# A 3×3 convolution in row pairs: the shared products of two blocks put side by side, and the last stores cut smaller

## The chip, the cores and the metric

The kernel runs on one core of a Trainium2 chip. The metric is the device time of one execution in microseconds (us); lower is better. Three timed runs of the kernel before gave 131.26, 131.46 and 131.46 us, a median of 131.46 us.

## The reference

`x` is 16 images of 64 channels, 64×64, fp32; `weight` is 128×64×3×3, nine tenths of it zeros; the output is 16×128×64×64 fp32 (33.6 MB). The reference skips zero weights, which changes nothing in the sum, so what is computed is a plain 3×3 convolution with zero padding:

```python
x_pad = np.pad(x, ((0, 0), (0, 0), (pad, pad), (pad, pad)), mode='constant')
...
output[b, co] += weight[co, ci, kh, kw] * x_pad[b, ci, kh:kh+h, kw:kw+w]
```

## The kernel before

**The arithmetic.** Two neighbouring output rows 2r and 2r+1 read the four input rows 2r−1 to 2r+2. With the kernel rows w0, w1, w2, both outputs hold the term w1·(x[2r]+x[2r+1]). The kernel computes this once, as the *shared product* P. What is left for the even row is E = w0·x[2r−1] + (w2−w1)·x[2r+1], done as one product over 128 partitions (two input rows of 64 channels each), and for the odd row likewise O = (w0−w1)·x[2r] + w2·x[2r+2]. The output rows are E+P and O+P.

**The tiling.** Images go in eight pairs; a pair's two images lie in partitions 0–63 and 64–127 of `xs` (bf16, converted by the loading DMA). A pair is cut into four blocks of 16 output rows, so there are 32 blocks, b = 0 to 31. For each block:

- `row_sum` (L106) adds neighbouring input rows into `ss[b % 2]`; POOL does it from block 2 on.
- `fill` (L108, copies at L130) builds `win[b % 2]`, in which each image takes 128 partitions: four half-windows per block. ACT copies two of them (both of image 1), POOL one, DVE one.
- TensorE runs three products of six matmuls each (L291). P is two images side by side, each on 64 of the 128 rows of the array, so its six matmuls run as three simultaneous pairs. E and O use all 128 rows, six matmuls one after the other. P goes to `ps_p[b % 2]` (two buffers), E to `ps_e`, O to `ps_o` (one buffer each).
- ACT copies `ps_p` to `pcs[b % 2]` (L211). DVE adds it to `ps_e` and then to `ps_o` and writes `os` (L244). I call these two the evictions of E and of O.
- After a pair's last block DVE writes a small `mark` (L252), on which the SP queue starts the store of `os`.

**The order.** There is no scheduler: every engine's program is written out by hand, with semaphores. TensorE runs a hardware loop of 16 turns, two blocks in a turn: P0 E0 O0 P1 E1 O1 (I number the blocks of a turn 0 and 1). Semaphores `s`, `xg`, `xd`, `xa` count row sums and window fills (by POOL, DVE, ACT), `e` and `o` count evictions, and `q` and `p` count finished products. At a turn's end TensorE takes two turns' worth of counts back with six semaphore decrements (L320):

```python
product(ps_e, lambda n: win[l][:, n, 0:16:2, :], EVEN,
    [[("e", l + 1), ("xg", l + 1), ("xd", l + 1)], [("xa", 2 * l + 2)]], "q")
product(ps_o, lambda n: win[l][:, n, 1:16:2, :], ODD, [[("o", l + 1)], []], "q")
```

So E of a block waits until E of the block before has been evicted; between the two lie O and P.

ACT's program for block b is: keep P(b) in `pcs`, fill one half-window of block b+1, fill one of block b+2. POOL's is: fill its half-window of block b, form the row sum of block b+1, and after blocks 4, 8, 12, 16 and 20 start a load of a later pair. DVE's is: evict E, evict O, fill its half-window of block b+2.

**The stores.** `os` has three buffers of a pair each. Pairs 0 to 6 are stored as one 4 MB DMA each (L145), pair 7 as two halves of 2 MB (L151), after blocks 29 and 31.

Of the kernel before, what the change touches and what calls it, by code (L numbers as in the profile page):

```python
# [17 lines left out]
def kernel(  # L18
# [11 lines left out]

    nc = tc.nc

    B, C_IN, H, W = x.shape
# [14 lines left out]
    def tiles(n, shape, dtype, name):  # L50
        return [pool.tile(shape, dtype, name=f"{name}{k}") for k in range(n)]
# [2 lines left out]
    win = tiles(2, [128, 2, 16, W], BF16, "win")  # L54
    os = tiles(N_O, [C_OUT, 2, H, W], FP32, "o")
    ss = tiles(2, [128, 8, W], BF16, "s")
    pcs = tiles(2, [128, 2, 8, W], FP32, "pc")
    w_sb = pool.tile([C_OUT, C_IN * KH * KW], FP32, name="w_sb")
    x_head = pool.tile([128, HEAD, W], FP32, name="x_head")
    ident = pool.tile([128, 128], BF16, name="ident")  # L60
    idle_rhs = pool.tile([128, 512], BF16, name="idle_rhs")
    w_bf = pool.tile([C_OUT, 3, 3, 2, C_IN], BF16, name="w_bf")
    wT = pool.tile([128, 3, 3, C_OUT], BF16, name="wT")
    mark = pool.tile([128, 1], FP32, name="mark")
    ps_p = [psum_pool.tile([128, 2, 8, W], FP32, name=f"ps_p{k}") for k in range(2)]
    ps_e = psum_pool.tile([128, 2, 8, W], FP32, name="ps_e")
    ps_o = psum_pool.tile([128, 2, 8, W], FP32, name="ps_o")
# [16 lines left out]
    def out_of(p):  # L84
        return out[2 * p : 2 * p + 2].rearrange("n o h w -> o n h w")
# [12 lines left out]

    X_LANDS = {0: 16, 1: 16, 2: 16, 3: 16, 4: 32, 5: 32, 6: 32, 7: 48}
    HEAD_R, HEAD_C, HEAD_Q = 6, 5, 3  # L100
    R_OF = {p: HEAD_R + p + 1 for p in range(NP - 1)}

    FIRST_E = ("q", HEAD_Q + 1)

    def row_sum(eng, b, rows):
        return eng.tensor_tensor(out=ss[b % 2], in0=rows[:, 0:16:2, :], in1=rows[:, 1:16:2, :], op=ADD)  # L106
# [1 line left out]
    def fill(copy, b, n, upper, name, *more):  # L108

        p, r0 = b // 4, 16 * (b % 4)  # L110
        src = slice(64 * n, 64 * n + 64)
        dst = slice(64 * upper, 64 * upper + 64)
        first = r0 - 1 + 2 * upper
        parts = []
        if p == 0 and first < HEAD:
            a, z = max(first, 0), min(first + 16, HEAD)
            parts.append((x_head[src, a:z, :], a - first))
        if p or first + 16 > HEAD:
            a, z = (first, first + 16) if p else (max(first, HEAD), first + 16)
            parts.append((xs[src, p, a + 1 : z + 1, :], a - first))  # L120
        for k, (rows, q) in enumerate(parts):
            waits = []
            if k == 0:
                waits.extend(more or [("q", HEAD_Q + 2 * (b - 2) + 2)] * (b >= 2))
                waits.extend([("xh", 16)] * (b < 2))
            if b in (1, 2) and k == 1:
                waits.append((x_sem(0), X_LANDS[0]))
            if b and b % 4 == 0:
                waits.append((x_sem(p), X_LANDS[p]))
            inst = after(copy(out=win[b % 2][dst, n, q : q + rows.shape[1], :], in_=rows), *waits)  # L130
            if k == len(parts) - 1:
                inst.then_inc(S(name), 1)

    with tc.tile_critical(no_gpsimd_drain=True):  # L134
        with nc.Block(no_gpsimd_drain=True) as block:  # L135

            @block.sync
            def _(sp):
                sp.dma_start(  # L139
                    out=w_sb, in_=weight.rearrange("o i kh kw -> o (i kh kw)")  # L140
                ).then_inc(S("w"), 16)
                sp.dma_start(out=x_head, in_=pair(0)[:, 0:HEAD, :]).then_inc(S("xh"), 16)
                for p in range(NP - 1):
                    after(
                        sp.dma_start(out=out_of(p), in_=os[p % N_O]), ("r", R_OF[p])  # L145
                    ).then_inc(S(f"st{p % N_O}"), 16)
                p = NP - 1
                for h in range(2):
                    rows = slice(32 * h, 32 * h + 32)
                    after(  # L150
                        sp.dma_start(  # L151
                            out=out_of(p)[:, :, rows, :], in_=os[p % N_O][:, :, rows, :]
                        ),
                        ("r", HEAD_R + NP + h),
                    ).then_inc(S("st7" if h else f"st{p % N_O}"), 16)

            @block.gpsimd
            def _(gp):
                def load(p, a, b, *waits):
                    after(  # L160
                        gp.dma_start(out=xs[:, p, a + 1 : b + 1, :], in_=pair(p)[:, a:b, :]), *waits  # L161
                    ).then_inc(S(x_sem(p)), 16)

                load(0, HEAD, H)
                gp.memset(ident, 0.0).then_inc(S("id"), 1)
                after(
                    gp.affine_select(
                        out=ident,
                        in_=ident,
                        compare_op=mybir.AluOpType.not_equal,  # L170
                        fill=1.0,
                        base=0,
                        pattern=[[-1, 128]],
                        channel_multiplier=1,
                    ),
                    ("id", 1),
                ).then_inc(S("id"), 1)
                for p in range(1, 4):
                    load(p, 0, H)
                load(4, 0, CUT)  # L180

                AT = {
                    4: (4, CUT, H, ("r", R_OF[0])),
                    8: (5, 0, H, ("r", R_OF[1])),
                    12: (6, 0, H, ("r", R_OF[2])),
                    16: (7, 0, 32, ("r", R_OF[3])),
                    20: (7, 32, H, ("r", R_OF[4])),
                }
                for b in range(1, NB):
                    fill(gp.tensor_copy, b, 0, 0, "xg", ("q", HEAD_Q + 2 * (b - 1) + 1))  # L190
                    if b + 1 < NB:
                        p, r0 = (b + 1) // 4, 16 * ((b + 1) % 4)
                        waits = [(x_sem(p), X_LANDS[p])] if r0 == 0 or b == 1 else []
                        if b == 1:
                            waits.append(("p", 2))
                        after(row_sum(gp, b + 1, xs[:, p, r0 + 1 : r0 + 17, :]), *waits).then_inc(S("s"), 1)
                    if b in AT:
                        load(*AT[b])

            @block.scalar  # L200
            def _(act):
                after(act.copy(out=w_bf[:, MID, :, 1, :], in_=w_row(1)), ("w", 16)).then_inc(S("c"), 1)  # L202
                act.copy(out=w_bf[:, EVEN, :, 0, :], in_=w_row(0)).then_inc(S("c"), 1)
                act.copy(out=w_bf[:, ODD, :, 1, :], in_=w_row(2)).then_inc(S("c"), 1)
                after(act.copy(out=wT[:, MID], in_=wps(MID)), ("q", 1)).then_inc(S("c"), 1)
                after(act.copy(out=wT[:, ODD], in_=wps(ODD)), ("q", 3)).then_inc(S("c"), 1)

                fill(act.copy, 0, 0, 0, "xg")
                fill(act.copy, 0, 1, 1, "xa")
                for b in range(NB):  # L210
                    after(act.copy(out=pcs[b % 2], in_=ps_p[b % 2]), ("p", b + 1)).then_inc(S("c"), 1)  # L211
                    if b == 0:
                        fill(act.copy, 1, 1, 1, "xa", FIRST_E)
                    if b + 1 < NB:
                        fill(act.copy, b + 1, 1, 0, "xa")
                    if b + 2 < NB:
                        fill(act.copy, b + 2, 1, 1, "xa")

            @block.vector
            def _(dve):  # L220
# [8 lines left out]
                after(dve.tensor_copy(out=wT[:, EVEN], in_=wps(EVEN)), ("q", 2)).then_inc(S("r"), 1)  # L229
                for b in range(2):  # L230
                    after(row_sum(dve, b, x_head[:, 16 * b : 16 * b + 16, :]), ("xh", 16)).then_inc(S("s"), 1)
                    fill(dve.tensor_copy, b, 0, 1, "xd")
                    if b == 0:
                        fill(dve.tensor_copy, b, 1, 0, "xa")
                for b in range(NB):
                    p, r0 = b // 4, 16 * (b % 4)
                    for k, src in enumerate((ps_e, ps_o)):
                        waits = [("q", HEAD_Q + 2 * b + k + 1)]
                        if k == 0:
                            waits.append(("c", HEAD_C + b + 1))  # L240
                            if b % 4 == 0 and p >= N_O:
                                waits.append((f"st{p % N_O}", 16 * (p // N_O)))
                        after(
                            dve.tensor_tensor(  # L244
                                out=os[p % N_O][:, :, r0 + k : r0 + 16 : 2, :], in0=src, in1=pcs[b % 2], op=ADD
                            ),
                            *waits,
                        ).then_inc(S("eo"[k]), 1)
                    if b + 2 < NB:
                        fill(dve.tensor_copy, b + 2, 0, 1, "xd")  # L250
                    if b % 4 == 3 or b == NB - 3:
                        dve.memset(mark, 0.0).then_inc(S("r"), 1)  # L252

            @block.tensor
            def _(pe):
# [46 lines left out]

                with pe.Fori(0, NB // TURN, 1):
                    for l in range(TURN):
                        product(ps_p[l], lambda n: ss[l], MID, [[("s", l + 1)], []], "p")
                        product(
                            ps_e,
                            lambda n: win[l][:, n, 0:16:2, :],
                            EVEN,
                            [  # L310
                                [("e", l + 1), ("xg", l + 1), ("xd", l + 1)],
                                [("xa", 2 * l + 2)],
                            ],
                            "q",
# [4 lines left out]
                    for name, n in (("s", 1), ("xa", 2), ("xd", 1), ("xg", 1), ("e", 1), ("o", 1)):  # L319
                        pe.sem_inc(S(name), -n * TURN)  # L320

    sixteen = nc.sync.to_reg(16)
    done = {f"st{k}": 16 * len([p for p in range(NP) if p % N_O == k]) for k in range(N_O)}
    for name in sorted(done, key=lambda k: (done[k], k)):
        nc.sync.wait_ge(S(name), nc.sync.to_reg(done[name]), synchronizes=[nc.sync.lower_ap(o[:]) for o in os])
    nc.sync.wait_ge(S("st7"), sixteen, synchronizes=[nc.sync.lower_ap(o[:]) for o in os])


# [28 lines left out]
```

## Time and profile before

| what | value |
|---|---|
| median of three runs | 131.46 us |
| the profiled execution's own time | 131.17 us |
| its span, first to last instruction | 129.4 us |
| PE busy | 117.0 us (90%) |
| ACT / DVE / POOL busy | 99.7 / 98.2 / 72.2 us |
| evictions, DVE (L244) | 64 of 1.22 us |
| keeps of P, ACT (L211) | 32 of 1.01 us |
| window fills (L130) | ACT 1.03, POOL 1.03, DVE 0.44 us in the mean |
| row sums, POOL (L106) | 30 of 1.15 us |
| stores of 4 MB, issue to landing | 15.6 us (median of 7) |
| stores of 2 MB, issue to landing | 8.7 us (median of 2) |

The profiled execution's time is 1.77 us above its span; this lies around the first and last instruction. PE's busy time is no measure of how near TensorE is to its limit, since matmuls overlap in it. The chain that ended last (PE 82% of the span) says more: from about 12 us to 119 us every step of it is a product on TensorE, and the next product follows it at once. The last 9 us of the span hold no engine's work, only DMA.

### The profile page before, as it was taken

What the parts mean: (1) busy time and instruction counts of PE and PEld (TensorE: products, weight loads), DVE (VectorE), ACT (ScalarE), POOL (GpSimd) and SP (SyncE); (2) the same over time, 40 slices, a digit from 0 to 9 for tenths busy, and PEclk for the clock granted to TensorE, in tenths of its full rate; (3) what the DMA queues carried; (4) which work ended last, traced back from release to release, by engine and by line L of the source; (5) the groups of instructions that cost most, each with busy time, mean ns of one, the idle gap of its engine ahead of it and who ended that gap; (6) DMA issues with size and microseconds to landing.
All of it is one profiled execution on the core that took longest, in us unless ns stands there. A gap on an engine that the chain in (4) does not pass through costs nothing.

```text
span 129.4 us, 1814 instructions
## 1 busy us (share of the span) xinstructions
PE 117.0 (90%) x599; PEld 44.0 (34%) x599; DVE 98.2 (76%) x116; ACT 99.7 (77%) x104; POOL 72.2 (56%) x78
## 2 busy tenths in 40 slices
PE   5997999999999999999999999999999999998000
PEld 2332343334333333333334333433333333333000
DVE  2589988888888888888888888888888888886200
ACT  3689988899888888888888889988888888863000
POOL 5406765675567666866667556755566666630000
PEclk9999999999999999999999999999999999999955
DMA  4999999999999999999999999999999916999994
GB/s 110 354 229 208 220 218 206 252 360 305 333 375 405 279 319 319 375 337 339 324 372 413 372 338 429 442 333 379 376 415 410 431 56 284 446 405 405 410 436 208
DMA packets 4179, 42.79 MB, mean 331 GB/s; under 512 B 336, under 2 KB 336, under 8 KB 1104
## 3 DMA queue, kind: packets, MB, share of 16 engines
q1 hardware_dynamic: 2736, 34.90, 65.8%
q0 software_dynamic: 1440, 7.86, 29.4%
q14 instruction: 3, 0.02, 0.0%
HBM read 17.07 MB, written 33.55 MB: 391 GB/s over the span
## 4 chain that ended last, share of the span: by engine, by line
PE 82%; DVE 5%; DMA 4%; issue 1%; SPq 0%; DVEq 0%
PE ps_e L291 34%; PE ps_o L291 31%; PE ps_p L291 17%; DMA x_head<-in_x_dram 4%; DVE win L130 2%; DVE o L244 2%; DVE s L106 1%; SPq L139 0%; SPq L352 0%; SPq L134 0%; DVEq L135 0%
## 5 line engine op out<-in xcount | busy, mean ns | idle before, releaser
L130 ACT COPY win<-xs 64x1024 bf16<-64x1024 bf16 (+2 forms) x61 | 62.7, 1028 | 12.3 <-PE ps_o L291 12.2
L244 DVE TENSOR_TENSOR o<-ps_e,pc 128x1024 f32<-128x1024 f32 x32 | 39.2, 1225 | 14.7 <-PE ps_e L291 14.4
L291 PE MATMUL ps_e<-win,wT 128*128 128x504 bf16 (+1 forms) x192 | 47.0, 381 | 0.7 <-DVE o L244 0.7
L130 POOL COPY win<-xs 64x1024 bf16<-64x1024 bf16 (+1 forms) x30 | 30.9, 1031 | 28.8 <-PE ps_e L291 28.8
L291 PE MATMUL ps_o<-win,wT 128*128 128x504 bf16 (+1 forms) x192 | 46.7, 380 | 0.0
L244 DVE TENSOR_TENSOR o<-ps_o,pc 128x1024 f32<-128x1024 f32 x32 | 39.2, 1224 | 1.5
L106 POOL TENSOR_TENSOR s<-xs 128x512 bf16<-128x512 bf16 x30 | 34.5, 1151 | 0.8 <-PE ps_p L291 0.8
L211 ACT COPY pc<-ps_p 128x1024 f32<-128x1024 f32 x32 | 32.4, 1012 | 2.0 <-PE ps_p L291 1.2
L291 PEld LDWEIGHTS ps_o<-win,wT 128*128 128x128 bf16 x192 | 18.8, 98 | 22.7 <-DVE o L244 0.2
L291 PE MATMUL ps_p<-s,wT 64*128 64x504 bf16 (+1 forms) x192 | 26.3, 380 | 0.0
L291 PEld LDWEIGHTS ps_e<-win,wT 128*128 128x128 bf16 x192 | 16.1, 97 | 29.6 <-issue 12.8
L130 DVE COPY win<-xs 64x1024 bf16<-64x1024 bf16 (+1 forms) x31 | 13.6, 439 | 0.9
L291 PEld LDWEIGHTS ps_p<-s,wT 64*128 64x128 bf16 x192 | 6.7, 94 | 17.4 <-issue 13.2
L161 POOL DMA_DIRECT2D xs<-in_x_dram x10 | 5.7, 571 | 7.1 <-DVE mark L252 6.1
L260 PE MATMUL ps_p<-idle_rhs 128*128 128x512 bf16 x14 | 5.2, 532 | 1.4 <-DVE idle_rhs L221 1.4
L130 POOL CAST win<-x_head 64x1024 bf16<-64x1024 f32 (+1 forms) x2 | 1.5, 772 | 6.2 <-PE ps_e L291 6.2
L130 ACT CAST win<-x_head 64x960 bf16<-64x960 f32 (+2 forms) x5 | 4.3, 862 | 0.6 <-DMA x_head<-in_x_dram 0.6
L260 PEld LDWEIGHTS ps_p<-idle_rhs 128*128 128x128 bf16 x14 | 1.7, 130 | 3.6 <-issue 1.9
L106 DVE TENSOR_TENSOR s<-x_head 128x512 bf16<-128x512 f32 x2 | 1.4, 692 | 0.9 <-DMA x_head<-in_x_dram 0.9
L130 DVE CAST win<-x_head 64x960 bf16<-64x960 f32 (+1 forms) x3 | 2.0, 665 | 0.1
L202 ACT ACT_TABLE_LOAD x1 | 1.3, 1283 | 0.9 <-SPq L134 0.9
L224 DVE CAST w_bf<-w_sb 128x192 bf16<-128x192 f32 x1 | 0.4, 385 | 2.0 <-DMA w_sb<-in_weight_dram 2.0
(23 smaller groups left out, 8.5 us busy)
## 6 DMA issues: line engine op xcount, KB each, us to landing
out_dram<-o SPq DMA_DIRECT2D x7, 4096.0 KB, 15.6
xs<-in_x_dram POOLq DMA_DIRECT2D x5, 1024.0 KB, 16.0
out_dram<-o SPq DMA_DIRECT2D x2, 2048.0 KB, 8.7
xs<-in_x_dram POOLq DMA_DIRECT2D x3, 512.0 KB, 13.2
x_head<-in_x_dram SPq DMA_DIRECT2D x1, 1024.0 KB, 5.6
xs<-in_x_dram POOLq DMA_DIRECT2D x1, 640.0 KB, 14.3
xs<-in_x_dram POOLq DMA_DIRECT2D x1, 384.0 KB, 21.2
w_sb<-in_weight_dram SPq DMA_DIRECT2D x1, 288.0 KB, 2.9
```

Source lines behind the costliest of these rows:

```text
L106: return eng.tensor_tensor(out=ss[b % 2], in0=rows[:, 0:16:2, :], in1=rows[:, 1:16:2, :], op=ADD)
L130: inst = after(copy(out=win[b % 2][dst, n, q : q + rows.shape[1], :], in_=rows), *waits)
L161: gp.dma_start(out=xs[:, p, a + 1 : b + 1, :], in_=pair(p)[:, a:b, :]), *waits
L202: after(act.copy(out=w_bf[:, MID, :, 1, :], in_=w_row(1)), ("w", 16)).then_inc(S("c"), 1)
L211: after(act.copy(out=pcs[b % 2], in_=ps_p[b % 2]), ("p", b + 1)).then_inc(S("c"), 1)
L224: after(dve.tensor_copy(out=w_bf[:, MID, :, 0, :], in_=w_row(1)), ("w", 16)).then_inc(S("r"), 1)
L244: dve.tensor_tensor(out=os[p % N_O][:, :, r0 + k : r0 + 16 : 2, :], in0=src, in1=pcs[b % 2], op=ADD),
L260: mm = pe.matmul(idle_ps, idle_rhs[:, 0:128], idle_rhs, start=True, stop=True)
L291: mm = pe.matmul(dst[:, n, :, c_lo:c_hi], wT[q, g, kw, :], src(n)[q, :, c_lo + kw - 1 : c_hi + kw - 1], start=(kw == KW_ORDER[0]), stop=(k ...
```

## The change

Two things are changed.

1. In each turn of TensorE's loop the shared products of both blocks come first: P0 P1 E0 O0 E1 O1 in place of P0 E0 O0 P1 E1 O1. The wait for the previous turn's last E eviction moves to P1, E0 waits for no eviction, and E1 still waits for that of E0. ACT, POOL and DVE's start are reordered to match: POOL does both row sums of the next turn after E0, and its fills after E1 and O1; ACT keeps P0, does one fill, keeps P1, then does three fills; `pcs` gets a third buffer. At the start, DVE forms both row sums before it fills windows, and ACT's first fill of block 1 and POOL's wait for other events than before.
2. Pair 6 is stored in two halves (after blocks 25 and 27), pair 7 as a half (block 29) and two quarters (blocks 30 and 31): eleven stores in place of nine. Each `mark` gets a column of its own.

```diff
-    pcs = tiles(2, [128, 2, 8, W], FP32, "pc")
+    pcs = tiles(3, [128, 2, 8, W], FP32, "pc")
...
-    R_OF = {p: HEAD_R + p + 1 for p in range(NP - 1)}
+    STORES = {4 * p + 3: (p, 0, H) for p in range(NP - 2)}
+    STORES |= {25: (6, 0, 32), 27: (6, 32, H), 29: (7, 0, 32), 30: (7, 32, 48), 31: (7, 48, H)}
+    R_OF = {b: HEAD_R + k + 1 for k, b in enumerate(STORES)}
+
+    def even_done(b):
+        return ("q", HEAD_Q + 2 * b + 1)
+
+    def odd_done(b):
+        return ("q", HEAD_Q + 2 * b + 2)
...
-                for p in range(NP - 1):
+                for b, (p, a, z) in STORES.items():
                     after(
-                        sp.dma_start(out=out_of(p), in_=os[p % N_O]), ("r", R_OF[p])
+                        sp.dma_start(out=out_of(p)[:, :, a:z, :], in_=os[p % N_O][:, :, a:z, :]),
+                        ("r", R_OF[b]),
                     ).then_inc(S(f"st{p % N_O}"), 16)
...
-                for b in range(1, NB):
-                    fill(gp.tensor_copy, b, 0, 0, "xg", ("q", HEAD_Q + 2 * (b - 1) + 1))
-                    if b + 1 < NB:
-                        p, r0 = (b + 1) // 4, 16 * ((b + 1) % 4)
...
-                        after(row_sum(gp, b + 1, xs[:, p, r0 + 1 : r0 + 17, :]), *waits).then_inc(S("s"), 1)
-                    if b in AT:
-                        load(*AT[b])
+                fill(gp.tensor_copy, 1, 0, 0, "xg", ("c", HEAD_C + 1))
+                for turn in range(NB // TURN - 1):
+                    if turn in AT:
+                        load(*AT[turn])
+                    b = TURN * turn
+                    for k in (2, 3):
+                        p, r0 = (b + k) // 4, 16 * ((b + k) % 4)
+                        waits = [even_done(b)] if k == 2 else []
+                        if k == 2 and (r0 == 0 or b == 0):
+                            waits.append((x_sem(p), X_LANDS[p]))
+                        after(row_sum(gp, b + k, xs[:, p, r0 + 1 : r0 + 17, :]), *waits).then_inc(S("s"), 1)
+                    fill(gp.tensor_copy, b + 2, 0, 0, "xg", even_done(b + 1))
+                    fill(gp.tensor_copy, b + 3, 0, 0, "xg", odd_done(b + 1))
...
-                for b in range(NB):
-                    after(act.copy(out=pcs[b % 2], in_=ps_p[b % 2]), ("p", b + 1)).then_inc(S("c"), 1)
+                def keep(b):
+                    after(act.copy(out=pcs[b % 3], in_=ps_p[b % 2]), ("p", b + 1)).then_inc(S("c"), 1)
+
+                for b in range(0, NB, TURN):
+                    keep(b)
                     if b == 0:
-                        fill(act.copy, 1, 1, 1, "xa", FIRST_E)
-                    if b + 1 < NB:
-                        fill(act.copy, b + 1, 1, 0, "xa")
+                        fill(act.copy, 1, 1, 1, "xa", ("xd", 2))
+                    fill(act.copy, b + 1, 1, 0, "xa")
+                    keep(b + 1)
                     if b + 2 < NB:
                         fill(act.copy, b + 2, 1, 1, "xa")
+                        fill(act.copy, b + 2, 1, 0, "xa")
+                        fill(act.copy, b + 3, 1, 1, "xa")
...
                 for b in range(2):
                     after(row_sum(dve, b, x_head[:, 16 * b : 16 * b + 16, :]), ("xh", 16)).then_inc(S("s"), 1)
-                    fill(dve.tensor_copy, b, 0, 1, "xd")
-                    if b == 0:
-                        fill(dve.tensor_copy, b, 1, 0, "xa")
+                fill(dve.tensor_copy, 0, 0, 1, "xd")
+                fill(dve.tensor_copy, 0, 1, 0, "xa")
+                fill(dve.tensor_copy, 1, 0, 1, "xd")
...
-                    if b % 4 == 3 or b == NB - 3:
-                        dve.memset(mark, 0.0).then_inc(S("r"), 1)
+                    if b in STORES:
+                        dve.memset(mark[:, b : b + 1], 0.0).then_inc(S("r"), 1)
...
                     for l in range(TURN):
-                        product(ps_p[l], lambda n: ss[l], MID, [[("s", l + 1)], []], "p")
+                        waits = [("s", l + 1)] + [("e", 1)] * l
+                        product(ps_p[l], lambda n: ss[l], MID, [waits, []], "p")
+                    for l in range(TURN):
                         product(
                             ps_e,
                             lambda n: win[l][:, n, 0:16:2, :],
                             EVEN,
                             [
-                                [("e", l + 1), ("xg", l + 1), ("xd", l + 1)],
+                                [("xg", l + 1), ("xd", l + 1)] + [("e", l + 1)] * l,
                                 [("xa", 2 * l + 2)],
                             ],
                             "q",
```

The loads of later pairs (table `AT`) are started at the beginning of turns 2, 4, 6, 8 and 10, on the same marks as before. The final waits of SP for the stores are written anew, on the same three semaphores as the stores raise.

## The prediction

> **What bounds the kernel now.** First the chain that ended last: two blocks of it.
>
> ```profile
> 47.35 1.40 PE ps_e L291 x6
> 48.75 1.30 PE ps_o L291 x6
> 50.05 0.76 PE ps_p L291 x6
> 50.80 1.40 PE ps_e L291 x6
> 52.20 1.30 PE ps_o L291 x6
> 53.50 0.76 PE ps_p L291 x6
> ```
>
> TensorE runs without a gap, 3.455 us per block, 6.91 per turn of two. Matmuls of O start 0.216 us apart, so six take 1.30. E needs 0.10 more than that. P's three pairs at 0.216 are 0.65, and it needs 0.76. So each change between the 64-row and 128-row shapes costs 0.10: four per turn.
>
> Second, the page's DMA share in 40 slices, then the windows and the timeline of the end:
>
> ```profile
> DMA  4999999999999999999999999999999916999994
> ```
>
> ```profile
> 104.00:107.60 3.60, 3.60 (x21) 1.39 (x19) 3.02 (x5) 3.14 (x4) 2.22 (x3) 1.00 0.00 0
> 107.60:117.60 10.00, 10.00 (x54) 3.72 (x53) 8.15 (x9) 7.75 (x8) 5.24 (x5) 1.00 0.99 419
> ...
> 122.60:127.80 5.20, 0.00 (x0) 0.00 (x0) 0.00 (x0) 0.00 (x0) 0.00 (x0) 0.50 1.02 425
> ```
>
> ```profile
> 107.16 0.37 SPq L145 DMA_DIRECT2D out_dram<-o  x1
> ...
> 114.07 0.37 SPq L151 DMA_DIRECT2D out_dram<-o  x1
> ...
> 120.32 0.06 DVE L252 MEMSET mark<- 128x1 f32 x1
> 120.43 0.37 SPq L151 DMA_DIRECT2D out_dram<-o  x1
> ```
>
> The last two columns of a window are the DMA share and GB/s. The DMA engines are full until about 104, idle for 3.6 us because pair 6 isn't issued before 107.16, and then full to 127.8. The end is thus set by 8.39 MB that start at 107.6 and move at 419–425 GB/s, 20.2 us, not by the last eviction (120.4).
>
> Third, the evictions and fills of DVE and POOL, and the one place where E waits for an eviction:
>
> ```profile
> 52.04 1.46 PE L291 MATMUL ps_o<-win,wT 128*128 128x512 bf16 x6
> ...
> 52.25 1.23 DVE L244 TENSOR_TENSOR o<-ps_e,pc 128x1024 f32<-128x1024 f32 x1 [0.37 <-PE ps_e L291]
> ...
> 10.08 1.32 POOL L130 CAST win<-x_head 64x1024 bf16<-64x1024 f32 x1 [5.26 <-PE ps_e L291]
> ...
> 10.43 1.01 DVE L130 COPY win<-xs 64x64 bf16<-64x64 bf16 x1
> ...
> 11.46 1.23 DVE L244 TENSOR_TENSOR o<-ps_e,pc 128x1024 f32<-128x1024 f32 x1
> ...
> 12.74 1.47 PE L291 MATMUL ps_e<-win,wT 128*128 128x512 bf16 x6 [0.68 <-DVE o L244]
> ```
>
> The eviction of E starts 0.21–0.23 after O's first matmul, takes 1.23, and E may go on 0.05 after its end (12.69 to 12.74).
>
> **TensorE in a steady turn.** The new order has two changes of shape instead of four: 2 × 0.10 = 0.205 saved with the exact period (6.91 − 30 × 0.2165 = 0.41 for four), 3.3 us over 16 turns. But between E0 and E1 now lies only O0, 1.30 us, where O and P (2.06) lay. E0's eviction returns 0.22 + 1.23 + 0.05 = 1.50 after O0's first matmul, so E1 waits 0.20: the saving is given back, 3.2 us over 16 turns. The weight load does not soften it: in the trace the first load of the O that waited for an eviction (ending 13.82) came at 13.87, after the release. I take the new turn as 6.91, the balance as 0.0, with bounds of −0.1 (a load that runs ahead) and +0.16 (the thin margins below).
>
> **The other engines in that turn** (0 = P0's start; P1 0.66, E0 1.40, O0 2.71, E1 4.21, O1 5.52, next P0 6.91). DVE: evict E0 2.93–4.16, O0 4.21–5.43, fill 5.46–5.88, E1 5.9–7.1, O1 7.05–8.3, fill to 8.7; P1 of the next turn (7.57) finds E1 evicted at 7.1. ACT: its fill released by the last O1 runs 0.15–1.19, keep P0 to 2.2 (needed 2.9), fill to 3.3 (needed 4.9), keep P1 to 4.3 (needed 5.9), two fills to 6.4. It works 2 × 1.01 + 4 × 1.04 = 6.2 of 6.9. POOL: load if any until 2.75 (mark at 1.87, then 0.31 and 0.57 as at 51.88 and 52.19), sums 2.94–5.24, fills at 5.75 and 7.05, each over 1 us ahead of its need. So all this is hidden; the third `pcs` buffer and the marks (0.06 each, two more) cost nothing.
>
> Two margins are thin. O1 waits for O0's eviction: end 5.43, release 0.05, weight load 0.10, against a stream that is free at 5.62: 0.04 to spare. And O1's wait now holds back the six decrements and the branch behind it in TensorE's queue: in the first turn these took from 13.88 to 15.16, 1.27 us (before, they ran far ahead). Now they end 0.12 before P0 is due. Cost 0, at most 0.06 + 0.10 per turn, 2.6 us in all.
>
> **The start.** P1 now precedes E0, so E0 starts at 9.18 instead of 8.55. DVE's small COPY at 10.43 took 1.01 us, ending with POOL's CAST; now POOL's CAST follows ACT's keep of P0 (9.08–10.09), runs 10.16–11.48 and holds the COPY until 11.51. E0's eviction: 11.54–12.77, E1 at 12.82 (before: 12.74). ACT's first fill of block 1 now waits for that COPY: 11.56, and with its three pieces (0.99 + 0.24 + 1.04) it ends at 13.84, while the second half of E1 wants it at 13.48: 0.4 lost. ACT is then late: keep P1 14.85, three fills to 18.17, keep P2 19.18. E2's eviction, which is due at 18.86, waits for it: 0.37 lost. By the third turn P0 starts at 23.2, against 22.35 before: 0.9. After that ACT has caught up. With 0.1 for the rest I take δ = 1.0 for every later event; bounds 0.2 (if POOL's CAST does not hold the COPY) and 1.5.
>
> **The stores.** Pair 6's first half is issued after block 25, at 107.16 − 6.91 + δ = 101.3, and follows pair 5's data at 103.8 without a gap: 2.10 MB at 425 GB/s are 4.93, to 108.7. The second half (108.2 with δ) ends at 113.7. Pair 7's half: issue 114.07 + δ, data 0.44 later (as 107.16 to 107.60), 114.5 + δ to 119.45 + δ. The quarters, issued at about 117.7 + δ (the last P0 at 112.2, and 5.5 to O0's eviction) and 120.43 + δ, follow at 2.47 each: 124.4 + δ. No row shows packets as small as theirs; 16 KB and 8 KB pieces moved at 419 and 425 GB/s, so 2.47 us is nearest, and 4.93 (no faster per piece than the halves) the far bound. Data ended at 127.8 before; the gain is 127.8 − 124.4 − 1.0 = 2.4, less 0.1 for the smaller pieces.
>
> **The sum.** 131.17 (the profiled time: span 129.4 and 1.77 around it) + 0.0 (TensorE's turns) + 1.0 (start) − 3.3 (stores) = 128.9. The median of the runs is 0.29 above the profiled time; I forecast 129.2 on that scale. With δ's bounds: 128.4 to 130.
>
> **Rivals.**
>
> *The weight load runs ahead of the wait.* E1's load of 0.10 is hidden in the wait: 16 × 0.1 = 1.6 less, 127.6. Against it: the load at 13.87. The Trainium skill, "TensorE: Matmul & The Clock Gate", step-by-step section, says that weight loads are pulled ahead of matmuls in flight when they go to the background buffer; by that rule this rival holds, but the row shows a load behind its semaphore.
>
> *POOL holds DVE's fill.* If POOL's sums run 0.5 late, its fill follows them directly; if DVE's COPY then finds POOL busy, as at 10.43, it waits to 6.8. E1's eviction runs 7.2–8.45, and P1, due at 7.57, starts at 8.5: 0.95 a turn. It decides from 0.5 us of lateness on. In the five turns with a load it costs 4.75, giving 134.0: slower. For it: the 1.01 us COPY. Against it: POOL is 0.2 early even then, and the COPY at 54.79 took 0.42 though POOL's sum (53.75, 1.16) overlapped its first 0.12. The Trainium skill, "SBUF — State Buffer", "Who interferes with whom", says that VectorE's fast copies and GpSimd lock each other out for a whole instruction; the trace agrees at 10.43, less clearly at 54.79.
>
> *The thin margins fail.* Both, each turn: 129.2 + 2.6 = 131.8, slightly slower. For it: 0.04 and 0.12 are within my reading of starts.
>
> *Quarters move slowly.* 2 × 2.46 more: 134.1. Against it: equal rates at 16 and 8 KB.
>
> **Numbers.** About 0.2% (0.26 us) is what a measurement can tell from no change. Forecast 0.62 (all of it faster), load ahead 0.12 (faster), POOL holds DVE 0.14 (0.03 of it in one turn only, still faster; 0.11 slower), margins 0.08 (0.02 faster, 0.03 same, 0.03 slower), slow quarters 0.04 (slower). Faster 0.79, same 0.03, slower 0.18. The range 127.2 to 131.8 holds the forecast, the load ahead, and the margins, about 0.8.
>
> **What would show it.** Right: TensorE's chain with P P E O E O, E1 waiting about 0.2 us for DVE on `ps_e`, turns of 6.9; PE's last product ending near 120.1; no idle slice of DMA before 114; data ending near 125.4; span near 127. Wrong: turns above 7.0 (the margins, or DVE's COPY above 0.42 us), turns of 6.8 or less (loads ahead), a start that is not 0.9 late, or a DMA rate that falls in the quarters.

## The result, and the profile after

The changed kernel took 133.16 us (median of four runs, 133.09 to 133.22), against 131.43 us before: a ratio of 1.0134, 95% interval 1.0117 to 1.0152. It is slower by 1.3%, where 129.2 us was forecast. The profiled execution took 133.21 us, its span is 131.4 us. (Some executions below were disturbed, the profiled ones with E1's wait first and with pair 7 in quarters among them; the ratios and the medians that I give leave them out.)

The chain that ended last, at the start and in a steady turn (start us, us, what):

```profile
10.40 3.23 DVE win L137
...
15.03 2.35 PE ps_e L299 x6
17.38 2.12 PE ps_o L299 x6
...
26.46 1.40 PE ps_p L299 x12
...
54.33 1.40 PE ps_p L299 x12
...
57.14 1.30 PE ps_o L299 x6
58.43 0.11 issue
58.55 1.46 PE ps_e L299 x6
...
61.30 1.40 PE ps_p L299 x12
```

The shared products now stand together (x12), and the two missing changes of shape can be seen: P and P take 1.40 where P alone took 0.76. A steady turn is 61.30 − 54.33 = 6.97 us, against 6.91 before. The third turn starts at 26.46. In the chain of the kernel before, it starts at 22.42:

```profile
22.42 0.76 PE ps_p L291 x6
```

The timeline of DVE and POOL in the first turn, and two windows, whose numbers are the busy times of TensorE, its weight loads, DVE, ACT and POOL, then the granted clock, the DMA share and GB/s:

```profile
10.40 3.23 DVE L137 COPY win<-xs 64x64 bf16<-64x64 bf16 x1
13.66 1.22 DVE L252 TENSOR_TENSOR o<-ps_e,pc 128x1024 f32<-128x1024 f32 x1
```

```profile
10.25 1.12 POOL L137 CAST win<-x_head 64x1024 bf16<-64x1024 f32 x1 [5.43 <-ACT pc L214]
11.34 2.24 POOL L113 TENSOR_TENSOR s<-xs 128x512 bf16<-128x512 bf16 x2
```

```profile
12.00:15.00 3.00, 0.01 (x1) 0.00 (x1) 2.97 (x3) 1.32 (x3) 1.58 (x2) 1.00 1.01 210
15.00:19.40 4.40, 4.37 (x12) 1.37 (x12) 2.66 (x3) 3.94 (x5) 1.15 (x2) 0.61 1.05 220
```

A copy of 64×64 values stood on DVE for 3.23 us and ended 0.05 after the end of the last of three POOL instructions (11.34 + 2.24 = 13.58). E0's eviction was queued behind it, and E1 behind that. TensorE did nothing from 12 to 15 us, and then got a clock of 0.61 in the mean of the next 4.4 us: eight of E1's and O1's twelve matmuls started 0.40 to 0.46 after the one before and not 0.216.

The DMA share of the profile page, and the window of the two quarters:

```profile
DMA  4999999519999999999999999999989999996995
```

```profile
124.50:129.50 5.00, 0.00 (x0) 0.00 (x0) 0.77 (x2) 0.00 (x0) 0.00 (x0) 0.86 1.02 406
```

The idle slices near 105 us are gone, as forecast. New ones stand near 25 to 29 us: the first store waits for the late start.

Where the 2.0 us of span come from, by the marks and turns of both traces:

| piece | before | after | difference |
|---|---|---|---|
| start of the third turn | 22.42 | 26.46 | +4.04 |
| 14 turns after it, by their lengths | 6.907 each | 6.967 each | +0.84 |
| last mark | 120.32 | 125.21 | +4.89 (the two above) |
| last mark to the span's end | 9.08 | 6.19 | −2.89 |

So the stores brought nearly what was forecast (2.9 of 3.3), and the start cost four times what was forecast.

### The profile page after: what moved, and what is told of

Its sections match the earlier page's. It is cut to its first block, busy times and chain, and to the rows that moved or that the text cites. A ratio compares the mean times of both kernels' runs of the same rounds, so it can differ in the third digit from the quotient of the medians.

```text
span 131.4 us, 1839 instructions
## 1 busy us (share of the span) xinstructions
PE 117.3 (89%) x599; PEld 45.4 (35%) x599; DVE 99.5 (76%) x118; ACT 99.5 (76%) x104; POOL 72.4 (55%) x78
## 4 chain that ended last, share of the span: by engine, by line
PE 82%; DVE 7%; DMA 4%; issue 2%; SPq 0%; DVEq 0%
PE ps_e L299 34%; PE ps_o L299 31%; PE ps_p L299 16%; DMA x_head<-in_x_dram 4%; DVE win L137 4%; DVE o L252 2%; DVE s L113 1%; SPq L146 0%; SPq L362 0%; SPq L141 0%; DVEq L142 0%
## 5 line engine op out<-in xcount | busy, mean ns | idle before, releaser
L299 PE MATMUL ps_e<-win,wT 128*128 128x504 bf16 (+1 forms) x192 | 47.7, 385 | 4.7 <-DVE o L252 3.0
L299 PE MATMUL ps_o<-win,wT 128*128 128x504 bf16 (+1 forms) x192 | 47.6, 385 | 0.0
L113 POOL TENSOR_TENSOR s<-xs 128x512 bf16<-128x512 bf16 x30 | 33.9, 1147 | 17.1 <-PE ps_e L299 17.1
L299 PE MATMUL ps_p<-s,wT 64*128 64x504 bf16 (+1 forms) x192 | 23.5, 378 | 0.6 <-DVE s L113 0.6
L137 DVE COPY win<-xs 64x1024 bf16<-64x1024 bf16 (+1 forms) x31 | 15.9, 511 | 0.9
L299 PEld LDWEIGHTS ps_p<-s,wT 64*128 64x128 bf16 x192 | 8.0, 94 | 15.1 <-issue 6.4
```

The costliest lines, as they stand in the source:

```text
L299: mm = pe.matmul(dst[:, n, :, c_lo:c_hi], wT[q, g, kw, :], src(n)[q, :, c_lo + kw - 1 : c_hi + kw - 1], start=(kw == KW_ORDER[0]), stop=(k ...
```

## The experiments

Theory A after this trace: the loss is at the start, where POOL shuts out one small copy and the clock falls in the pause. Theory B: the loss is in every turn, from E1's wait for E0's eviction. The kernel before, timed along with these runs, took 131.2 to 131.3 us.

**POOL's first CAST waits for DVE** (`h` is raised by a `memset` behind DVE's fill of block 1):

```diff
-                fill(gp.tensor_copy, 1, 0, 0, "xg", ("c", HEAD_C + 1))
+                fill(gp.tensor_copy, 1, 0, 0, "xg", ("c", HEAD_C + 1), ("h", 1))
```

> The changed kernel, but POOL's first CAST (its fill of block 1) also waits until DVE has made its fill of block 1, so that DVE's small COPY meets no POOL instruction. Theory A (the loss is at the start: the COPY is shut out by POOL's three instructions in a row, and the clock falls in the pause): E0's eviction starts near 10.8 us and not 13.66, TensorE's clock stays at 1.0, the third turn begins 4.1 us earlier, and the time is 133.2 - 4.1 = 129.1 us. Theory B (the loss is in every turn, by E1's wait for E0's eviction): what the start gains is under 1 us, 132.3 or more.

Measured: 128.89 us, ratio 0.9827 (0.9811 to 0.9844). Its timeline of DVE at the start:

```profile
10.42 0.17 DVE L137 COPY win<-xs 64x64 bf16<-64x64 bf16 x1
...
10.77 1.23 DVE L253 TENSOR_TENSOR o<-ps_e,pc 128x1024 f32<-128x1024 f32 x1
...
13.32 1.07 DVE L137 COPY win<-xs 64x1024 bf16<-64x1024 bf16 x1
```

And POOL's:

```profile
10.85 1.03 POOL L137 CAST win<-x_head 64x1024 bf16<-64x1024 f32 x1 [6.02 <-DVE mark L243]
11.85 2.26 POOL L113 TENSOR_TENSOR s<-xs 128x512 bf16<-128x512 bf16 x2
14.05 0.43 POOL L137 CAST win<-x_head 64x64 bf16<-64x64 f32 x1
```

The copy takes 0.17 us when no POOL instruction runs, and E0's eviction starts at 10.77. The clock row of its profile page stays at 9 in every slice but the last, and the third turn starts at 22.29. 4.3 us come back by one wait on an engine that is itself not on the path. Theory A holds for most of the loss.

**POOL's first row sum waits, its CAST does not:**

```diff
+                        if k == 2 and b == 0:
+                            waits.append(("h", 1))
                         after(row_sum(gp, b + k, ...
```

> The changed kernel, but POOL's first row sum (not its CAST) waits until DVE has made its fill of block 1. If a DVE COPY is shut out as long as POOL instructions follow one another: the COPY is now held by the CAST alone, about 1.0 us as in the kernel before, E0's eviction starts near 11.5 us, the clock stays at 1.0, and the prediction's 1.0 us for the start comes out: 133.2 - 3.1 = 130.1 us. If the COPY waits for something else that ends at 13.6 us (a load, a semaphore): 133.2.

Measured: 129.80 us, ratio 0.9854 (0.9753 to 0.9956). DVE's timeline:

```profile
10.56 1.01 DVE L137 COPY win<-xs 64x64 bf16<-64x64 bf16 x1
```

And POOL's:

```profile
10.40 1.12 POOL L137 CAST win<-x_head 64x1024 bf16<-64x1024 f32 x1 [5.55 <-ACT pc L216]
11.86 2.27 POOL L113 TENSOR_TENSOR s<-xs 128x512 bf16<-128x512 bf16 x2 [0.33 <-DVE mark L245]
```

The same copy: 0.17 us beside an idle POOL, 1.01 when it meets one POOL instruction, 3.23 when it meets three in a row. With the CAST alone in its way the third turn starts at 23.26, 0.84 after the old order's, where the prediction worked out 0.9 for the start. Of the 0.84, 0.25 is no effect of the order: `x_head` landed at 7.23 in this execution, and at 6.98 in that of the kernel before. So the prediction's chain is right for the kernel that it assumed, one in which no POOL instruction stands behind the CAST; that it meets 0.9 so closely is in part luck.

The Trainium skill, "SBUF — State Buffer", "Who interferes with whom", says that VectorE's fast copies and GpSimd exclude each other, and that the first to issue holds the ports for its whole instruction. The trace agrees that the copy is shut out, but not for one instruction alone: the row sums that issued after the waiting copy went ahead of it, twice. Nor is that a rule. With the CAST waiting (the lines above), DVE's copy of 13.32, which takes 0.42 alone, met POOL's second row sum. It ended at 14.39, 0.28 after that sum, although a CAST of POOL stood directly behind; this CAST took 0.43 and not the 0.23 of the changed kernel. What decides who goes first is open.

**Idle matmuls in the pause** (the first turn is written out ahead of the loop):

```diff
+                        if warm and l == 0:
+                            keep_busy(warm, ("c", HEAD_C + 1))
...
+                turn(warm=12)
+                with pe.Fori(0, NB // TURN - 1, 1):
+                    turn()
```

> The changed kernel with twelve idle matmuls (on zeros, into a bank of ps_p that is free then) in the pause between O0 and E1 of the first turn, which is written out ahead of the loop for it. The COPY still takes 3.23 us. If it is the pause of 3.0 us that lowers the clock: E1 still starts near 15.0, but E1, O1 and the way to the next P take 2.9 us with ACT's wait and not 4.4, the clock stays at 1.0, 133.2 - 1.4 = 131.8 us. If the clock falls for another reason, or its fall costs nothing later: 133.2.

Measured: 132.0 us, ratio 1.0045 (1.0001 to 1.0088). The timeline of TensorE and a window:

```profile
12.15 2.75 PE L268 MATMUL ps_p<-idle_rhs 128*128 128x512 bf16 x12
15.33 1.71 PE L299 MATMUL ps_e<-win,wT 128*128 128x512 bf16 x6 [0.43 <-DVE o L252]
...
18.27 1.47 PE L299 MATMUL ps_p<-s,wT 64*128 64x512 bf16 x12
```

```profile
15.30:18.30 3.00, 2.89 (x14) 1.05 (x16) 2.56 (x3) 2.95 (x4) 1.16 (x2) 1.00 1.02 213
```

The copy was still shut out, and E1 started as late, but at full clock: E1 to the next P took 2.94 us and not 4.40. So the pause did lower the clock. Of the 1.46, about 1.2 arrive at the end, since ACT, late too, then holds E2's eviction. The Trainium skill, "TensorE: Matmul & The Clock Gate", Part 1, gives free-running windows of about 3.4 us, and half the clock after one that was idle. In the changed kernel the low clock lasted 3.41 us, from 15.50 to 18.91, which agrees in length. But the pause was 3.0 us, and E1 had run for 0.47 us when the clock fell: a pause shorter than the 3.4 us that its advice there ("HAM oscillation") names was enough.

**E1's wait for the eviction put first in its list:**

```diff
-                                [("xg", l + 1), ("xd", l + 1)] + [("e", l + 1)] * l,
+                                [("e", l + 1)] * l + [("xg", l + 1), ("xd", l + 1)],
```

> The changed kernel with E1's three waits in another order, the one for E0's eviction first, as in the kernel before. In the changed kernel E1's first matmul starts 0.147 us after E0's eviction ends, behind an extra wait instruction in TensorE's queue that takes 0.051 us; in the kernel before the one such wait took 0.056. If the place of the wait in the list decides: 0.09 less in each of 15 turns, turns of 6.88 instead of 6.97, 133.2 - 1.35 = 131.8 us. If the way from DVE to TensorE costs that much wherever the wait stands: 133.2.

Measured: 131.4 us (median of seven runs, 130.7 to 132.3), ratio 1.002 (0.9988 to 1.0052), 1.8 under the changed kernel, where 1.35 was expected. Not all of this need be the wait. In five of the seven the mean granted clock is 0.987 to 0.990, as high as in the runs with the CAST waiting (0.986 to 0.991), whose trace shows no fall at the start; in all four runs of the changed kernel it is 0.972 to 0.974. So in these five the pause seems to have cost no clock, though no trace of them was kept; the other two took 132.2 and 132.3 us. What the edit did to a turn is in the timelines. First the changed kernel, then this one:

```profile
64.14 1.22 DVE L252 TENSOR_TENSOR o<-ps_e,pc 128x1024 f32<-128x1024 f32 x1 [1.13 <-PE ps_e L299]
...
65.48 0.56 PEld L299 LDWEIGHTS ps_e<-win,wT 128*128 128x128 bf16 x4 [0.58 <-issue]
65.51 0.81 PE L299 MATMUL ps_e<-win,wT 128*128 128x512 bf16 x3
```

```profile
71.27 1.22 DVE L252 TENSOR_TENSOR o<-ps_e,pc 128x1024 f32<-128x1024 f32 x1 [0.96 <-PE ps_e L299]
...
72.55 0.55 PEld L299 LDWEIGHTS ps_e<-win,wT 128*128 128x128 bf16 x4 [0.51 <-DVE o L252]
72.55 0.82 PE L299 MATMUL ps_e<-win,wT 128*128 128x512 bf16 x3
```

From the eviction's end to E1 it is 0.15 us in the one and 0.06 in the other, and turns go from 6.967 to 6.893 us. In the changed kernel the records of TensorE's queue show a wait instruction of 0.051 us of its own between the two; where the late event stands first, the weight load itself waits for it. So the excess of the turns is the place of one wait in a list. The same rows answer the first rival: E1's weight load comes after the eviction's end (65.36 and 72.49) in both, and doesn't run ahead of the wait. With the wait first, the turn is 0.014 under the old one: the saved changes of shape (0.205) and E1's wait cancel, as the prediction had it, and theory B is right that E1 waits in every turn, but the wait is paid for.

**Both mends together:**

> The changed kernel with both mends: POOL's first CAST waits for DVE's fill of block 1, and E1's wait for the eviction stands first. The two should add up: 128.9 - 15 x 0.074 (turns of 6.893 instead of 6.967) = 127.8 us, under the kernel before with the new stores alone (128.5). If the store chain sets the end by itself by then: 128.5.

Measured: 129.1 us (three runs, 128.0 to 129.4), ratio 0.977 (0.962 to 0.992). The time doesn't tell whether they add up. In the profiled execution they do: the turns are 6.89, and though `x_head` landed 1.0 us later than in the profile of the first mend alone (6.7 against 5.7 us from its issue), the last mark is at 120.96 against 121.04. So 1.1 us were won, and lost to a late first load in that execution.

**The stores alone, in the old order** (the diff's second part on the kernel before):

> The kernel before with the eleven smaller stores alone, products in the old order. By the chain of bytes in the prediction (nothing moved by the start): data end at 124.4 instead of 127.8, 131.4 - 3.3 = 128.1 us. By what the changed kernel shows from its last mark to the end of the span (6.2 instead of 9.1 us): 131.4 - 2.9 = 128.5. If the smaller stores bring nothing by themselves: 131.4.

Measured: 128.50 us (128.22 to 128.58), ratio 0.9792 (0.9768 to 0.9815): 2.7 less. The old order with these stores beats the new order with them by 4.7, about what the start and the turns cost in the table (4.9).

**The order alone, with the old stores:**

> The changed kernel with the nine old stores: the new order alone. Theory A and B both give the changed kernel plus what the stores bring: 133.2 + 2.9 = 136.1 us, and 4.8 above the kernel before; together with the run of the stores alone it says whether the two parts add up. If the smaller stores only shift the end because the work ends later: 133.2 to 134.

Measured: 135.8 us, ratio 1.0351 (1.0333 to 1.0368): 4.6 more than before. The two parts add up: 4.6 − 2.7 = 1.9, and the whole change costs 1.7.

**Evictions in halves**, so that E1 waits for half an eviction (with both mends, and five decrements moved ahead of O1):

```diff
-                                out=os[p % N_O][:, :, r0 + k : r0 + 16 : 2, :], in0=src, in1=pcs[b % 3], op=ADD
...
+                        for n in range(2):
...
+                                    out=os[p % N_O][:, n, r0 + k : r0 + 16 : 2, :],
+                                    in0=src[:, n],
+                                    in1=pcs[b % 3][:, n],
...
+                                [("e", 3)] * l + [("xg", l + 1), ("xd", l + 1)],
+                                [("e", 2 * l + 2), ("xa", 2 * l + 2)],
```

> The kernel with both mends, and with each eviction cut into two halves (one image each), so that E1's first three matmuls wait for half an eviction only; five of TensorE's six decrements move ahead of O1. If E1's wait is then gone, the saved changes of shape are left: turns of 6.70 instead of 6.89, and TensorE alone would give 127.8 - 2.9 = 124.9 us; but the stores of pairs 5 to 7 (12.6 MB from about 94.4 us on at 425 GB/s end at 124 us) hold the end at about 127. If four half evictions cost DVE more than it has to spare (4 x 0.69 + 0.42 = 3.2 of 3.35 us a block), turns of 6.9 or more and 128 or more.

Measured: 129.40 us, ratio 0.9866 (0.9851 to 0.9880). The chain has a steady turn as expected, 71.05 − 64.35 = 6.70 us, with E1 following O0 at once:

```profile
64.35 1.40 PE ps_p L304 x12
...
67.16 1.30 PE ps_o L304 x6
68.45 1.30 PE ps_e L304 x6
...
71.05 1.40 PE ps_p L304 x12
```

This is the whole saving of the two changes of shape, 0.21 a turn. The time did not follow: a copy was shut out once more, now in the third turn, by the second of two row sums and by two fills:

```profile
26.07 2.27 POOL L113 TENSOR_TENSOR s<-xs 128x512 bf16<-128x512 bf16 x2
28.27 2.02 POOL L137 COPY win<-xs 64x1024 bf16<-64x1024 bf16 x2
```

```profile
27.84 2.74 DVE L137 COPY win<-xs 64x1024 bf16<-64x1024 bf16 x1
```

**The same, with POOL's loads after its row sums:**

```diff
-                    if turn in AT:
-                        load(*AT[turn])
                     b = TURN * turn
...
+                    if turn in AT:
+                        load(*AT[turn])
                     fill(gp.tensor_copy, b + 2, 0, 0, "xg", even_done(b + 1))
```

> The split kernel with one edit: in the five turns with a load, POOL starts the load after its two row sums and not ahead of them. In the split kernel the sums of turn 2 ran 26.07 to 28.34 because the load ahead of them waited for a mark; DVE's COPY (ready at 27.84) met them, then POOL's two fills, and took 2.74 us. If that is the lock of the first turn again: the sums end before the COPY, it takes 0.42, the third block pair no longer loses 2.3 us, and the time falls by 1.5 to 2.3 from 129.5, to about 127.5, where the stores hold it. If the COPY is late for another reason: 129.5.

Measured: 128.02 us (127.74 to 128.41), ratio 0.974 (0.969 to 0.979). The copy in question is back at 0.43 us (28.38), and 1.4 us are won, where 1.5 to 2.3 were expected. That is the prediction's rival, POOL holding DVE's fill behind a late load, seen and taken away, though in one turn of a kernel with split evictions and not in the changed kernel.

**Pair 7 in quarters, old order** (`28: (7, 0, 16), 29: (7, 16, 32), 30: (7, 32, 48), 31: (7, 48, H)`):

> The old order with the new stores, and pair 7 in four quarters, after blocks 28 to 31. With the half and two quarters the DMA share falls to 0.81 between 114 and 118 us, 0.8 us of 16 idle engines, since pair 7's first half is issued at 114.1 only. If that gap is what is left to win: data end 0.8 to 1.0 earlier, 128.5 - 0.9 = 127.6 us. If 4 KB pieces move more slowly than 8 KB ones, two more quarters give it back: 128.5 or more.

Measured: 128.85 us, ratio 0.9817 (0.9763 to 0.9871). A miss: nothing was won over 128.50. In its trace the quarters moved at 406 GB/s (118 to 124 us). Against the 425 of a half before, the two added quarters lose 0.24 us by that, an estimate; the rest of the 0.9 that was expected is open.

**Pair 0 in halves as well, new order and old** (`1: (0, 0, 32), 3: (0, 32, H)`):

> The kernel of the later load, with pair 7 in quarters and pair 0 stored in halves (after blocks 1 and 3), so that the stores begin some 7 us earlier, in the stretch near 20 to 25 us where DMA has idle slices. If the stores hold the end from first to last, the idle time filled there is won at the end: 126.5 us. If TensorE sets the end: the same as without, 127.5. Smaller stores beside the loads could also delay the loads that follow: more than 127.5.

> The old order with pair 7 in quarters and pair 0 in halves. If TensorE's order (last eviction at 120.4) sets the end of the old order once pair 7 is in quarters, the earlier start of the stores brings nothing: as with the quarters alone, 127.6 us. If the stores set it: 126.6.

Measured: 127.80 us, ratio 0.9732 (0.9683 to 0.9782), in the new order (with split evictions, POOL's loads after its sums, and pair 7 in quarters); 127.86 us, ratio 0.9734 (0.967 to 0.980), in the old order. They are the lowest two medians, and equal within their spread. Both are 1.3 over what was expected of stores that set the end. In the old order it is 1.0 under the quarters alone, the step that was expected of them. In the new order it is 0.2 under 128.02, inside the spread of that run, so there the earlier stores aren't shown to have won anything. The DMA share in the new order and in the old, and a window of the end in the new:

```profile
DMA  4999999999999999999999999999999999999992
```

```profile
DMA  4999999999999999999999999999999999999995
```

```profile
118.00:122.00 4.00, 0.00 (x0) 0.00 (x0) 0.00 (x0) 0.00 (x0) 0.00 (x0) 0.87 1.02 417
```

In both, the DMA engines are busy from the second slice to the last but one. In the new order TensorE's work is over some 3 us earlier (last mark 117.21 against 120.33), and both kernels end at 126.0 to 126.1 us: with these stores, a TensorE that is done 3 us sooner won nothing. That the 42.8 MB of loads and stores now hold both orders is my reading of these rows; no run moved fewer bytes.

## Why the prediction was wrong

- **The start, +1.0 forecast, +4.0 measured: the step that failed.** The prediction had POOL's CAST hold DVE's COPY to 11.51, and E0's eviction start at 11.54. It did not ask what POOL has queued behind the CAST: the term was priced at one POOL instruction, and three stood there. In the kernel before, POOL's row sum came 0.83 us after the CAST, so its trace could only show a copy that is let in after one instruction. The change put two sums directly behind it, and the copy ended at 13.63. That is 2.1 us; E1 running at half clock after the pause is 1.5 more, 1.2 of it at the end; the rest is in the 0.84 that remains with the CAST alone (0.25 of it a later first load). The upper bound of 1.5 was drawn around the wrong event.
- **The rival was named and misplaced.** "POOL holds DVE's fill" was the right mechanism on the right two engines, and it was looked for in the steady turns, where every copy of the trace after took its 0.42 us. The first turn, where the prediction had POOL and DVE overlap as well, was given the price of the old trace.
- **The clock did not enter the sum.** A pause of 0.80 us, near the one forecast, cost no clock (the row sums waiting: clock 1.0 throughout the start); a start that is late by 2 us more brings it in.
- **TensorE's turn, 0.0 forecast, +0.84 measured in 14 turns.** The saving of 0.205 and E1's wait of 0.20 were right to 0.02 (6.893 with the wait first), and the weight load stayed behind the wait, as it had it. Missed was that the release of a wait costs 0.06 or 0.15 us, by whether the late event is the load's own wait or a wait instruction's ahead of it; the diff shows it, since it moves `e` from the first place to the last.
- **The thin margins held.** In the steady turns of the trace O1 starts 1.29 after E1 and the next P 1.39 after O1, as without a wait, so neither O0's eviction nor the six decrements cost anything.
- **The stores, −3.3 forecast, −2.9 with the new order, −2.7 alone.** The chain of bytes was right. The quarters moved at 406 GB/s and not 425, which is 0.24 us over the two, where 0.1 was allowed for (in the new order's last kernel quarters moved at 417, so the size of a piece alone doesn't set the rate); of the rest I have no account.

The first of these decides: with the CAST alone in the copy's way, the kernel took 129.8 us, 0.6 over the forecast.

## What to carry to other kernels

When an edit moves one engine's work in time, follow the work of every engine that shares a resource with it through the first turns as well as the steady one, and for each overlap ask what is queued behind the blocker, not only how long the blocker is, since what follows may go first. A price from a trace holds only for the neighbours that it had there. And before making a stage faster, ask what the end is bound by: here stores that start earlier were worth more (131.2 to 127.9 in the old order) than all that was won on TensorE.

## What the runs showed of the hardware

- A DVE copy that is ready while POOL works is shut out, and POOL instructions that follow can go ahead of it: 0.17 us alone, 1.01 against one instruction, 3.23 against three; another, of 0.42, took 2.74 against three. They don't always: with a small CAST of POOL directly behind a row sum, a copy of 0.42 took 0.97 to 1.07 in five traces, was let in at the sum's end, and the CAST took 0.43 and not 0.23.
- In the changed kernel's steady turns a copy that had started first kept its 0.42 us, and POOL's next instruction beside it its 1.03; they overlapped by 0.08 only.
- A pause of 3.0 us on TensorE was followed by 3.41 us at half clock; twelve idle matmuls in it kept the clock at 1.0. By the mean clocks, the same pause seems to have cost no clock in five runs with E1's wait first.
- Of several waits on one matmul, the one that ends last should stand first: 0.06 instead of 0.15 us from the event to the matmul.
- Two products in the 64-row shape next to each other cost no change of shape between them (1.40 for both, 0.76 for one); with no wait in the way, each pair of changes saved is 0.21 us.
